# Fewer projection products kept back at the seam between the recurrence and the attention, and the first attention loads on GpSimd

## The chip, the core and the metric

The kernel runs on one core of a Trainium2 chip. Its engines are TensorE (PE in the profile, with its weight loads as PEld), VectorE (DVE), ScalarE (ACT), GpSimd (POOL) and SyncE (SP, which here only issues DMA transfers). Each engine takes its instructions in the order in which they stand in its program. The metric is the time of one execution on the device in microseconds (us). A profiled execution gives the trace that is read below; the timed runs are made without a profile.

## The reference, cut to what matters

The reference is one encoder block for 1024 tokens of width 1024, in float32. The parts around the change are the input projection, whose columns feed all branches, the first branch (a neighbourhood attention with six heads) and the second (a recurrence over time, run in both directions):

```python
h = rms_norm(x, norm_mix_g[l])
(na_q, na_k, na_v, p_r, p_k, p_v, lat_w, lat_a, lat_g, mem_q,
 gate_na, gate_rw, gate_mem) = split_columns(h @ w_in[l])
y_na = neighborhood_attention(to_heads(na_q, NA_HEADS), ...)
y_rw = rwkv7_bidirectional(p_r, p_k, p_v, lat_w, lat_a, lat_g, ...)
y_mem = memory_attention(mem_q, rms_norm(mem, norm_mem_g[l]), w_mem_kv[l])
merged = (jax.nn.sigmoid(gate_na) * (y_na @ w_branch_na[l])
          + jax.nn.sigmoid(gate_rw) * (y_rw @ w_branch_rw[l])
          + jax.nn.sigmoid(gate_mem) * (y_mem @ w_branch_mem[l]))
x = x + merged @ w_out[l]
x = x + expert_choice_ffn(rms_norm(x, norm_ffn_g[l]), ...)
```

The recurrence is a chain: every step needs the state that the step before it left.

## The kernel before, in words

The kernel works through six stages: (1) norms and the projections that the recurrence needs; (2) the recurrence, from about 350 to 826 us of the span, in which TensorE fills its waits with the other projections; (3) the attention with the group norm of the recurrence beside it, from about 853 us; (4) the merge of the branches; (5) the output projection with the router; (6) the 16 experts, whose weights are streamed.

**Products in high and low parts.** Each float32 operand is split into a high part (a copy by ScalarE, line 231) and a low part (a subtraction by VectorE, line 232), and a product is the sum of three matmuls: high by high, low by high, high by low.

**The filler.** `fill_gen` (lines 676 to 737) makes the 35 column blocks of the input projection that the recurrence does not need ("jobs"). A job has two halves of 512 tokens; each half is 24 matmuls of 128x128 by 128x512 (line 728), so that there are 1680 of these *products* in all. A step of the generator is one product. When the third product of the next half has been issued, the half before it is copied out of its PSUM bank by ScalarE (`evac`, line 716) and stored by SyncE (line 717). The two banks `acc` are used in turn, so a half cannot begin before the one two halves back has been copied out. At the seventh k step of a job's first half the weights of the next job are split (`prepw`) and those of the one after it are fetched (`load`, line 687).

**The order of the recurrence is written out by hand.** For each of its 16 units (`units`, 128 tokens of one direction) three generators are stepped round by round: `chain` of this unit (13 rounds), `t_inverse` of the next one (a triangular inverse, 31 column steps on GpSimd, then DMA transfers out to `tdr` on line 575 and back into the tile `Tbd` on line 579) and `prep` of the one after. After each round some products of the filler follow: 7 in a round until two units are left, and from there `(NFILL * 48 - RES - tail) / 28`, where `tail` is the count when that part begins (1503). With `RES` = 80 that is 3.46 a round, and 80 products are left when the last round is over; after the chain's last own matmul (line 664), 89 follow. In `chain`, line 634 is the first matmul that reads `Tbd`.

**The seam.** Lines 831 to 835 then call `na_load(0)`, the loads for the first pair of heads: its query `q` (512 KB, in two halves), the bias table of the first half of the rows (`bias_load(0)`, 960 KB) and its values `VC` (896 KB), all by SyncE, whose queue is taken in order. `na_load` goes on with the split of the query: the high parts by ScalarE (line 809), the low ones by VectorE (line 810). Only then does the loop issue the products that are left, with their copies and the split of the last job's weights. Behind them the attention begins with transposes of `VC` (line 820), scores (line 981), bias and maximum (line 987) and the exponential (line 930). `bias_load(1)` and `bias_load(2)` and the loads of the second pair of heads (`q`, `kt`, line 794) are issued by SyncE around these.

**The pool.** `ap_` holds all tiles of the attention. It takes the memory of the recurrence's pool `rp`, and a tile of it waits until the tiles that lay in its place are no longer used. Tiles are laid out in the order of their first mention.

Of the kernel before, what the change touches and what calls it, by code (L numbers as in the profile page):

```python
# [25 lines left out]
F32 = mybir.dt.float32  # L26
# [31 lines left out]
NB_ = dict(s=2, tr=2, gn=1, av=1)  # L58
PSEQ = "E A | B X | x0 | r0 | s0 o0 x1 | r1 | s1 o1 L | | T"
PRI, XTB = None, 3  # L60
NFILL, PER_ROW, TROW, PFB, RES, PRE, ROW0 = 35, 7.0, 8, 2, 80, 26, 10


def shape_constants():
# [96 lines left out]
def block_kernel(ctx: ExitStack, tc: tile.TileContext, T, out, dbg=None, upto=99):  # L161
    nc = tc.nc
    dbg = dbg or {}
    V, A, G, PE, SP = nc.vector, nc.scalar, nc.gpsimd, nc.tensor, nc.sync
# [4 lines left out]
    def scratch(name, shape):  # L169
        if name in dbg:  # L170
            return dbg[name]
        t = dram.tile(list(shape), F32, name=name)
        return t
# [24 lines left out]
    pna = scratch("pna", (6, 128, S))  # L198
    pvc = scratch("pvc", (3, 128, 16 * WSUM))
# [87 lines left out]
    with tc.tile_pool(name="wp", bufs=1, side="right", reuse_waits="tile") as wp:  # L287
# [14 lines left out]
        with (tc.tile_pool(name="qp", bufs=1, side="right", reuse_waits="tile") as qp,  # L302
# [41 lines left out]
            def mixed(d, pf, om, mu, name, bufs):  # L344
                cur, sh = (slice(1, S + 1), slice(0, S)) if d == 0 else (slice(S, 0, -1), slice(S + 1, 1, -1))
                m = qp.tile([128, S], F32, name=name, bufs=bufs)
                A.activation(m, pf[:, cur], AF.Copy, scale=om)
                V.scalar_tensor_tensor(m, pf[:, sh], mu, m, op0=OP.mult, op1=OP.add)
                return m
# [3 lines left out]
            for d in range(2):  # L353
                m = mixed(d, pf, omw[:, d:d + 1], P_("muwa", d), f"ml{d}", 1)
# [12 lines left out]
            for j in range(3):  # L367
# [3 lines left out]
                for d in range(2):  # L371
                    m = mixed(d, kf, omu[:, d * 9 + 3 + j:d * 9 + 4 + j], P_("mu", d * 9 + 3 + j), f"K{d}", 1)
# [8 lines left out]
                for d in range(2):  # L381
# [7 lines left out]
                    rb = qp.tile([128, 8, 2, 64], F32, name="rb", bufs=1)  # L389
# [19 lines left out]
                for d in range(2):  # L409
                    m = mixed(d, rf, omu[:, d * 9 + j:d * 9 + j + 1], P_("mu", d * 9 + j), "R", 1)  # L410
# [3 lines left out]
                for d in range(2):  # L414
                    m = mixed(d, vf, omu[:, d * 9 + 6 + j:d * 9 + 7 + j], P_("mu", d * 9 + 6 + j), "VV", 1)
# [353 lines left out]

    yctx = ExitStack()  # L770
    ap = yctx.enter_context(tc.tile_pool(name="ap_", bufs=1, side="right", reuse_waits="tile"))
    na, bias = {}, {}
    grid = lambda t: t.rearrange("p (r c) -> p r c", c=64)

    def bias_load(m):
        if m < 6:
            bias[m] = ap.tile([128, 2, BOFF[3]], F32, name="bias", bufs=3)
            SP.dma_start(bias[m], T["rpb"][m // 2, m % 2])

    def na_load(j):  # L780
        q = ap.tile([128, S], F32, name="q", bufs=2)
        VC = ap.tile([128, 16 * WSUM], F32, name="VC", bufs=1)
        qb = [ap.tile([128, 2, 4, 128], F32R, name=f"qb{v}", bufs=2) for v in "hl"]
        KT = kt0 if j == 0 else [(ap if j == 1 else nq).tile([128, S], F32R, name=f"KT{v}") for v in "hl"]
        na[j] = [KT, qb]
        if j == 0:
            SP.dma_start(q[:, 0:512], pna[j][:, 0:512])
            bias_load(0)
            SP.dma_start(VC, pvc[j])
            SP.dma_start(q[:, 512:], pna[j][:, 512:])  # L790
        else:
            kt = ap.tile([128, S], F32, name="kt", bufs=1)
            for t, src in ((q, pna[j]), (kt, pna[3 + j]), (VC, pvc[j])):
                SP.dma_start(t, src)
        VW = []
        for c0, ct in zip(COL0S, CTYPE):
            at, w = sum(v.shape[1] for v in VW), NCOL[ct]
            VW.append(VC[:, at:at + 16 * w])
        if j:
            yield  # L800
            yield
            for v in (slice(0, 512), slice(512, 1024)):
                A.activation(KT[0][:, v], kt[:, v], AF.Copy)
                G.tensor_tensor(KT[1][:, v], kt[:, v], KT[0][:, v].bitcast(F32), op=OP.subtract)
                yield
        for rh in range(2):
            hi, lo = (v[:, rh].rearrange("p g (r c) -> p g r c", c=16) for v in qb)
            src = q[:, 512 * rh:512 * rh + 512].rearrange("p (r g c) -> p g r c", r=8, g=4)
            A.activation(hi, src, AF.Copy)
            (G if j else V).tensor_tensor(lo, src, hi.bitcast(F32), op=OP.subtract)  # L810
            if j or rh:
                yield
        VT = ap.tile([128, 4, 4, 128], F32, name="VT", bufs=2)
        na[j].append(VT)
        for c2 in (0, 2):
            p = abank("s")
            for cg in (c2, c2 + 1):
                w = NCOL[CTYPE[cg]]
                for i in range(4):
                    PE.transpose(p[:4 * w, cg - c2, i * 128:(i + 1) * 128], VW[cg][:, 4 * i * w:4 * (i + 1) * w], ident)  # L820
            yield p, VT, c2
# [9 lines left out]
    with tc.manual_schedule():  # L831
        start = na_load(0)
        next(start)
        for _ in range(NFILL * 48 + 1 - done):
            next(fill)
    pre_ctx.close()
    pctx.close()
    aps_ctx = ExitStack()
# [311 lines left out]
    with tc.tile_pool(name="mt", bufs=1, side="right", reuse_waits="tile") as mt:  # L1150
        wq = [None, None]
        for dt_ in range(KD):
            wh, wl = wbr(dt_)
            for t0 in range(0, S, 512):
# [3 lines left out]
                m = mt.tile([128, 512], F32, name="m", bufs=1)  # L1158
                for b, (k0, n) in enumerate(((0, 3), (6, 2), (3, 3))):
# [6 lines left out]
                    else:  # L1166
                        w = mt.tile([128, 512], F32, name="u", bufs=2)
# [212 lines left out]
    with tc.tile_pool(name="eps", bufs=1, space=PSUM, reuse_waits="tile") as ps, tc.manual_schedule():  # L1380
# [93 lines left out]
        for s_ in range(steps + 1):  # L1474
# [6 lines left out]
            if s_:  # L1481
                pt = bank("tr", 2)
# [86 lines left out]
```

## Time and profile before

| what | value |
|---|---|
| median of 3 timed runs | 2369.76 us (2368.66 to 2372.98) |
| the profiled execution | 2379.35 us, its span 2377.6 us |
| busy share of the span | PE 95%, DVE 70%, ACT 55%, POOL 26% |
| mean granted clock of TensorE in that execution | 0.97 |

The span is the part of the profiled execution in which the engines work; the 1.75 us around it are the launch. "PEclk" is TensorE's granted clock as a share of 2.4 GHz: 1.00 is 2.4 GHz and 0.50 is 1.2 GHz, the two levels that appear; a value between them is a stretch with both. In rows of the timeline, the columns are the start in us, the duration in us, the engine, the line, the operation, output and input, the count, and in brackets the idle time of the engine before it with what ended that. SPq is SyncE's DMA queue; its row is the issue of a transfer, and the time that it stands there can include the wait for the transfer's conditions.

### The profile page before, as it was taken

Reading aid. Unit: us, or ns where it says so; the run is one execution under the profiler, and the core shown is the slowest. Engines: PE = TensorE matmul, PEld = TensorE weight load, DVE = VectorE, ACT = ScalarE, POOL = GpSimd, SP = SyncE. Lnnn points to the kernel's source line nnn. Section 1 sums busy time; section 2 is a strip of 40 time slices with the busy share of each in tenths; the row PEclk is TensorE's granted clock in tenths of the full one; section 3 lists DMA queues with packets and bytes.
Section 4 is the critical chain, followed back from the end, with each engine's and each line's share of the span. In section 5 each row is a group of like instructions: output and inputs, shape, how many; then the busy total and the mean of one; then the engine's idle time right before and its main releaser. Section 6 shows DMA issues by size and latency. Waiting matters only on the chain.

```text
span 2377.6 us, 33501 instructions
## 1 busy us (share of the span) xinstructions
PE 2247.3 (95%) x12494; PEld 1816.5 (76%) x12494; DVE 1665.2 (70%) x2030; ACT 1312.9 (55%) x1588; POOL 623.1 (26%) x1266
## 2 busy tenths in 40 slices
PE   7999999999999989899957999999999999999996
PEld 6677787877878756577846888888888888888885
DVE  6556556556656246564267898889888888888887
ACT  5554233333433346521235777777777777777775
POOL 1000567666666325443040000000000000000001
PEclk9999999999999998899978999999999999999998
DMA  6335444443442262075296999999999999999995
GB/s 236 151 142 208 114 115 128 127 115 105 132 123 76 80 224 98 17 233 182 93 351 243 375 379 389 385 391 383 394 381 380 380 389 386 389 387 390 379 349 195
DMA packets 196643, 594.19 MB, mean 250 GB/s; under 512 B 53376, under 2 KB 100736, under 8 KB 147328
## 3 DMA queue, kind: packets, MB, share of 16 engines
q1 hardware_dynamic: 189856, 568.62, 64.8%
q0 software_dynamic: 4752, 17.30, 2.7%
q10 hardware_dynamic: 1872, 6.13, 0.7%
q8 instruction: 98, 1.61, 0.3%
q14 instruction: 65, 0.53, 0.1%
HBM read 522.61 MB, written 69.39 MB: 249 GB/s over the span
## 4 chain that ended last, share of the span: by engine, by line
PE 51%; DVE 3%; POOL 1%; ACT 1%; issue 1%; DMA 1%; POOLq 0%; ACTq 0%; DVEq 0%
PE y L1436 14%; PE g L1424 5%; PE g L1425 5%; PE g L1427 5%; PE u L1424 5%; PE u L1425 5%; PE u L1427 5%; PE acc L235 2%; PE acc L237 1%; PE acc L236 1%; PE tr L1484 1%; POOL m L1169 1%; PE tr L1414 1%; PE pl L1256 1%; DVE ye L1342 0%
## 5 line engine op out<-in xcount | busy, mean ns | idle before, releaser
L1401 DVE TENSOR_TENSOR ewl<-raw,ewh 128x2048 fp32r<-128x2048 f32 x380 | 849.8, 2284 | 5.3 <-ACT ewh L1396 5.3
L1396 ACT ACTIVATE ewh<-raw 128x2048 fp32r<-128x2048 f32 x380 | 720.7, 1914 | 112.7 <-PE u L1425 85.2
L1443 POOL DMA_INDIRECT acc<-ye,idx x15 | 43.4, 2893 | 949.0 <-DVE ye L1442 872.1
L728 PE MATMUL acc<-hhi,wh 128*128 128x512 f32 x560 | 226.9, 405 | 3.7 <-ACT po L716 3.7
L728 PE MATMUL acc<-hhi,wl 128*128 128x512 f32 x560 | 226.9, 405 | 0.3 <-DVE wl L232 0.3
L728 PE MATMUL acc<-hlo,wh 128*128 128x512 f32 x560 | 226.5, 405 | 0.0
L568 POOL TENSOR_TENSOR tmul<-tinv,blk 96x60 f32<-96x60 f32 (+24 forms) x496 | 171.3, 345 | 147.8 <-DMA blk<-ldr 110.2
L1424 PE MATMUL g<-ewh,xh 128*128 128x512 f32 x512 | 206.0, 402 | 0.0
L1424 PE MATMUL u<-ewh,xh 128*128 128x512 f32 x512 | 202.2, 395 | 0.0
L1425 PE MATMUL g<-ewh,xl 128*128 128x512 f32 x512 | 200.2, 391 | 0.0
L1425 PE MATMUL u<-ewh,xl 128*128 128x512 f32 x512 | 199.5, 390 | 0.0
L570 POOL TENSOR_TENSOR tinv<-tinv,tmul 96x60 f32<-96x60 f32 (+24 forms) x496 | 178.5, 360 | 38.9
L1436 PE MATMUL y<-ewh,ah 128*128 128x512 f32 x512 | 137.9, 391 | 0.7 <-ACT ah L231 0.7
L1436 PE MATMUL y<-ewh,al 128*128 128x512 f32 x512 | 137.7, 391 | 0.0
L1436 PE MATMUL y<-ewl,ah 128*128 128x512 f32 x512 | 137.6, 391 | 0.0
L1427 PE MATMUL g<-ewl,xh 128*128 128x512 f32 x512 | 137.4, 390 | 0.0
L1427 PE MATMUL u<-ewl,xh 128*128 128x512 f32 x512 | 137.0, 389 | 0.0
L728 PEld LDWEIGHTS acc<-hhi,wh 128*128 128x128 f32 x560 | 107.0, 191 | 24.5 <-ACT po L716 4.1
L728 PEld LDWEIGHTS acc<-hhi,wl 128*128 128x128 f32 x560 | 106.9, 191 | 20.9 <-DVE wl L232 0.6
L728 PEld LDWEIGHTS acc<-hlo,wh 128*128 128x128 f32 x560 | 107.1, 191 | 20.6
L231 ACT ACTIVATE ah<-tr 128x512 fp32r<-128x512 f32 x64 | 38.4, 599 | 143.6 <-PE tr L1484 143.6
L232 DVE TENSOR_TENSOR wl<-wraw,wh 128x1024 fp32r<-128x1024 f32 (+1 forms) x60 | 75.5, 1263 | 54.6 <-ACT wh L231 54.5
(316 smaller groups left out, 4377.5 us busy)
## 6 DMA issues: line engine op xcount, KB each, us to landing
raw<-in_wg_dram SPq DMA_DIRECT2D x128, 1024.0 KB
raw<-in_wu_dram SPq DMA_DIRECT2D x128, 1024.0 KB
raw<-in_wd_dram SPq DMA_DIRECT2D x128, 1024.0 KB
wraw<-in_wt_dram SPq DMA_DIRECT2D x46, 512.0 KB
pt<-pz SPq DMA_DIRECT2D x16, 768.0 KB
pgt<-po SPq DMA_DIRECT2D x48, 256.0 KB
gt<-pgt SPq DMA_DIRECT2D x16, 768.0 KB
blk<-ldr SPq DMA_DIRECT2D x64, 96.0 KB
```

The source lines that it names most:

```text
L232: V.tensor_sub(lo, src, hi.bitcast(F32))
L235: PE.matmul(out_, lh, rh, start=(k_ == 0), stop=False)
L568: G.tensor_tensor(tm[:, 0:m, 0:n], tt[:, 0:m, j:j + 1].to_broadcast([4 * NB, m, n]), lt[:, j, None, j + 1:32].to_broadcast([4 * NB, m, n]) ...
L570: G.tensor_tensor(tt[:, 0:m, j + 1:32], tt[:, 0:m, j + 1:32], tm[:, 0:m, 0:n], op=OP.add)
L728: PE.matmul(p, l[:, k], r[:, k, s0:s0 + 512], start=(k == 0 and i == 0), stop=(k == KD - 1 and i == 2))
L1396: A.activation(hi, raws[seq[n]], AF.Copy)
L1401: V.tensor_sub(lo, raws.pop(seq[n]), his[seq[n]].bitcast(F32))
L1424: PE.matmul(p, xh[:, 4 * b + k], wh[:, k], start=(b == 0 and k == 0), stop=False)
L1425: PE.matmul(p, xl[:, 4 * b + k], wh[:, k], start=False, stop=False)
L1427: PE.matmul(p, xh[:, 4 * b + k], wl[:, k], start=False, stop=(b == 1 and k == 3))
L1436: PE.matmul(py[n], l[:, 2 * b + k], r[:, k, n * 512:(n + 1) * 512], start=(f == 0 and b == 0 and i == 0 and k == 0), stop=(f == 3 and b == ...
L1443: G.indirect_dma_start(out=acc[:, :], out_offset=bass.IndirectOffsetOnAxis(ap=idx[:, e:e + 1], axis=0), in_=ye, in_offset=None, compute_op ...
```

## The change

`RES` goes from 80 to 48: the last two units get 4.61 products a round in place of 3.46, and fewer are left behind the recurrence. The first three loads of the attention (`q` now in one piece, the first bias table, `VC`) are issued by GpSimd in place of SyncE. `na_load` has a `yield` behind the loads, so that the query's split is called later: after 29 of the products that are left (`n == RES // 2 + 4`). The pool mentions its tiles `sb`, `pt`, `y`, `rb` and `rq` first, so that these lie in the first places and `q`, the bias tables and `VC` elsewhere.

```diff
-NFILL, PER_ROW, TROW, PFB, RES, PRE, ROW0 = 35, 7.0, 8, 2, 80, 26, 10
+NFILL, PER_ROW, TROW, PFB, RES, PRE, ROW0 = 35, 7.0, 8, 2, 48, 26, 10
...
     ap = yctx.enter_context(tc.tile_pool(name="ap_", bufs=1, side="right", reuse_waits="tile"))
+    for nm, w, n in (("sb", 768, 4), ("pt", 768, 2), ("y", 128, 3), ("rb", 128, 2), ("rq", 128, 2)):
+        ap.tile([128, w] if w == 128 and nm != "rq" else [128, 2, w // 2], F32, name=nm, bufs=n)
...
-            SP.dma_start(bias[m], T["rpb"][m // 2, m % 2])
+            (SP if m else G).dma_start(bias[m], T["rpb"][m // 2, m % 2])
...
         if j == 0:
-            SP.dma_start(q[:, 0:512], pna[j][:, 0:512])
+            G.dma_start(q, pna[j])
             bias_load(0)
-            SP.dma_start(VC, pvc[j])
-            SP.dma_start(q[:, 512:], pna[j][:, 512:])
+            G.dma_start(VC, pvc[j])
...
+        yield
         if j:
-            yield
             yield
...
         next(start)
-        for _ in range(NFILL * 48 + 1 - done):
+        for n in range(NFILL * 48 + 1 - done):
             next(fill)
+            if n == RES // 2 + 4:
+                next(start)
```

What this moves is seen in the built programs. First TensorE in the last unit of the recurrence, from behind its first key transposes to the first matmul that reads `Tbd`. Before:

```order
L728 MATMUL acc<-hhi,wh 128x512
L728 MATMUL acc<-hhi,wl 128x512
L728 MATMUL acc<-hlo,wh 128x512
L626 MATMUL ch<-Gst,AR 64x64 x6
L728 MATMUL acc<-hhi,wh 128x512
L728 MATMUL acc<-hhi,wl 128x512
L728 MATMUL acc<-hlo,wh 128x512
L634 MATMUL ch<-u0s,Tbd_1662 128x64 x3
```

And now:

```order
L728 MATMUL acc<-hlo,wh 128x512
L728 MATMUL acc<-hhi,wh 128x512
L728 MATMUL acc<-hhi,wl 128x512
L728 MATMUL acc<-hlo,wh 128x512
L728 MATMUL acc<-hhi,wh 128x512
L626 MATMUL ch<-Gst,AR 64x64 x6
L728 MATMUL acc<-hhi,wl 128x512
L728 MATMUL acc<-hlo,wh 128x512
L728 MATMUL acc<-hhi,wh 128x512
L728 MATMUL acc<-hhi,wl 128x512
L728 MATMUL acc<-hlo,wh 128x512
L634 MATMUL ch<-u0s,Tbd_1662 128x64 x3
```

Ten products stand here where six stood. Counted over the program, the last unit but one has 14 products more (60 for 46), the last unit 12 more (46 for 34, 4 of them ahead of line 634), and 63 follow the last matmul of the chain where 89 did.

Then GpSimd, from the end of its last triangular inverse (lines 568 and 570) on. Before:

```order
L568 TENSOR_TENSOR tmul<-tinv,blk 96x8
L570 TENSOR_TENSOR tinv<-tinv,tmul 96x8
L804 TENSOR_TENSOR KTl<-kt,KTh 128x512
L873 TENSOR_TENSOR y_8836<-y_8836,y_8838 128x512
L874 TENSOR_TENSOR b_8840<-b_8840,b_8842 128x512
```

And now:

```order
L568 TENSOR_TENSOR tmul<-tinv,blk 96x8
L570 TENSOR_TENSOR tinv<-tinv,tmul 96x8
L789 DMA q<-pna 128x1024
L780 DMA bias<-in_rpb_dram 128x1920
L791 DMA VC<-pvc 128x1792
L805 TENSOR_TENSOR KTl<-kt,KTh 128x512
```

The three loads stand directly behind the inverse. By the conditions in the built program, `q` waits for nothing later than the preparation of an earlier unit, the bias table for the last unit's second key transposes (line 596), and `VC` for the matmuls behind those (line 600).

Last ScalarE, from the last copy of the recurrence (`ysb`) to the first copies of the attention. Before:

```order
L670 ACTIVATE ysb<-ch 128x3x64
L809 ACTIVATE qbh<-q 128x512 x2
L231 ACTIVATE wh<-wraw 128x1024
L716 ACTIVATE po<-acc 128x512 x4
L829 COPY VT<-s 96x512
```

And now:

```order
L670 ACTIVATE ysb<-ch 128x3x64
L716 ACTIVATE po<-acc 128x512 x2
L810 ACTIVATE qbh<-q 128x512 x2
L716 ACTIVATE po<-acc 128x512
L830 COPY VT<-s 96x512
```

The query's split has two copies of the filler ahead of it and one behind it; the split of the last job's weights (line 231) has gone up into the last unit. On SyncE, the bias tables 1 and 2 now stand behind the store of the first of these copies, and `q` and `kt` of the second pair of heads behind the store of the second.

## Rows read from the trace of the kernel before

**Rows 1.** The page: busy time of TensorE, with its share of the span and its instructions, and of the other engines.

```profile
PE 2247.3 (95%) x12494; PEld 1816.5 (76%) x12494; DVE 1665.2 (70%) x2030; ACT 1312.9 (55%) x1588; POOL 623.1 (26%) x1266
```

**Rows 2.** Stretches of 10 us around the seam: start and end, length, busy us of PE, PEld, DVE, ACT and POOL with the instructions, granted clock, busy share of the DMA engines, GB/s.

```profile
800.00:810.00 10.00, 6.87 (x45) 5.39 (x44) 0.35 (x1) 3.22 (x8) 0.00 (x0) 0.80 0.43 116
810.00:820.00 10.00, 10.00 (x86) 7.95 (x86) 2.75 (x9) 2.78 (x7) 0.00 (x0) 0.69 0.01 2
...
830.00:840.00 10.00, 6.27 (x27) 4.64 (x25) 2.43 (x3) 3.18 (x5) 0.00 (x0) 1.00 1.01 411
```

**Rows 3.** The timeline of TensorE from the end of the recurrence to the attention.

```profile
802.72 0.40 PE L728 MATMUL acc<-hlo,wh 128*128 128x512 f32 x1
...
806.25 1.51 PE L634 MATMUL ch<-u0s,Tbd 128*128 128x64 f32 x6 [3.13 <-DMA Tbd<-tdr]
...
813.88 0.91 PE L600 MATMUL tr<-cst,XV 128*64 128x64 f32 x12
...
827.68 0.39 PE L728 MATMUL acc<-hhi,wl 128*128 128x512 f32 x1
...
835.39 0.39 PE L728 MATMUL acc<-hlo,wh 128*128 128x512 f32 x1
839.46 0.49 PE L728 MATMUL acc<-hhi,wh 128*128 128x512 f32 x1 [3.69 <-ACT po L716]
840.24 0.80 PE L728 MATMUL acc<-hhi,wl 128*128 128x512 f32 x1 [0.28 <-DVE wl L232]
...
852.38 0.39 PE L728 MATMUL acc<-hlo,wh 128*128 128x512 f32 x1
853.51 1.95 PE L820 MATMUL s<-cst,VC 128*96 128x128 f32 x16 [0.74 <-ACT po L716]
```

**Rows 4.** The timeline of SyncE's DMA queue in the same stretch.

```profile
798.27 3.27 SPq L575 DMA_DIRECT2D tdr<-tinv  x4
803.05 1.78 SPq L579 DMA_DIRECT2D Tbd<-tdr  x4
...
805.36 0.48 SPq L687 DMA_DIRECT2D wraw<-in_wt_dram  x1
...
826.65 0.37 SPq L673 DMA_DIRECT2D yrw<-ysb  x1
827.12 0.43 SPq L787 DMA_DIRECT2D q<-pna  x1
...
828.57 0.42 SPq L790 DMA_DIRECT2D q<-pna  x1
...
840.80 1.21 SPq L794 DMA_DIRECT2D kt<-pna  x1
```

**Rows 5.** The timeline of ScalarE.

```profile
831.18 0.63 ACT L809 ACTIVATE qbh<-q 128x512 fp32r<-128x512 f32 x1 [4.56 <-DMA q<-pna]
837.35 0.63 ACT L809 ACTIVATE qbh<-q 128x512 fp32r<-128x512 f32 x1 [5.53 <-DMA q<-pna]
837.89 1.04 ACT L231 ACTIVATE wh<-wraw 128x1024 fp32r<-128x1024 f32 x1
838.83 1.06 ACT L716 ACTIVATE po<-acc 128x512 f32<-128x512 f32 x2
...
859.11 0.61 ACT L803 ACTIVATE KTh<-kt 128x512 fp32r<-128x512 f32 x1
...
862.34 1.06 ACT L876 ACTIVATE lg<-lg 128x1024 f32<-128x1024 f32 x1 [1.41 <-DMA lg<-plat]
```

**Rows 6.** Stretches cut at the falls of the clock (columns as in rows 2); the last is at the beginning of the attention.

```profile
806.20:816.50 10.30, 10.24 (x44) 8.54 (x44) 0.35 (x1) 2.45 (x6) 0.00 (x0) 0.51 0.28 86
...
840.20:843.70 3.50, 3.46 (x8) 2.78 (x9) 0.00 (x0) 0.00 (x0) 0.00 (x0) 0.51 1.03 311
...
864.00:871.00 7.00, 6.67 (x30) 4.22 (x30) 1.81 (x7) 4.71 (x14) 6.34 (x7) 0.51 0.80 298
```

**Rows 7.** What TensorE waited for in all of the recurrence and up to 830 us: total us, times, the longest.

```profile
PE sc L237 <- DVE rsl L232: 5.9, 16, 0.8
PE ch L634 <- DMA Tbd<-tdr: 3.1, 1, 3.1
```

**Rows 8.** The timeline of GpSimd at the end of its last triangular inverse, and its next instruction.

```profile
798.03 0.22 POOL L570 TENSOR_TENSOR tinv<-tinv,tmul 96x8 f32<-96x8 f32 x1
859.80 1.27 POOL L804 TENSOR_TENSOR KTl<-kt,KTh 128x512 fp32r<-128x512 f32 x1 [61.56 <-PE tr L995]
```

**Rows 9.** A load that GpSimd issues in this kernel, the gather of 128 rows of 4 KB for the first expert, and the matmul that waits for it.

```profile
1259.05 1.22 POOL L1406 DMA_INDIRECT xe<-h2d,idx  x1 [10.33 <-DVE tvT L1359]
...
1263.45 1.97 PE L1414 MATMUL tr<-cst,xe 128*128 128x128 f32 x8 [4.92 <-DMA xe<-h2d,idx]
```

**Rows 10.** The recurrence up to 800 us, and two stretches of 2 us: start and end, length, busy us of PE, granted clock, busy share of the DMA engines, GB/s.

```profile
350.00:800.00 450.00, 442.33 (x3504) 1.00 0.41 113
...
800.00:802.00 2.00, 2.00 (x27) 1.00 0.17 25
...
836.00:838.00 2.00, 0.00 (x0) 1.00 1.00 419
```

**Rows 11.** What TensorE waited for at the beginning of the attention, in the stretch from 820 to 900 us.

```profile
PE tr L995 <- ACT pt L999: 2.8, 3, 2.1
...
PE tr L995 <- DVE st L933: 1.3, 1, 1.3
```

## The prediction, made before the result was known

> **What bounds the kernel now.** I read the page first. TensorE is busy for 2247.3 of 2377.6 us [rows 1], so almost any time is won where it stands still or runs slowly, and the others matter where it waits for them. The stretches of 10 us come next: around the seam TensorE is busy for 6.87 us in one of them and for 6.27 in another, and the granted clock is 0.80 in the first of these and 0.69 in the full stretch behind it [rows 2], where it was 1.00 over the 450 us before [rows 10]. The timelines then say why, engine by engine, and cutting the stretches at the falls of the clock gives what these cost.
>
> There are two stalls, and each is followed by a slow stretch. In the first, TensorE ends a product at 803.12 us (802.72 and 0.40) and stands for 3.13 us until `Tbd` has landed [rows 3]. The inverse is ready at 798.25 [rows 8], SyncE writes it out from 798.27 and begins to read it back at 803.05 [rows 4]: a path of DMA alone, and too few products lie beside it. The wait is the only one of its kind in the recurrence [rows 7]. Behind it the clock is at its lower level, 1.2 GHz, for about 10 us (0.51 over 10.30 us) [rows 6]. In the second, TensorE stands for 3.69 us at 839.46 for a copy `po` of ScalarE, and 0.28 us more for the low part of the weights [rows 3]. ScalarE was not busy but held: it stood for 4.56 and 5.53 us before the two query copies, for `q`, and the copies and weight split that the filler needs stood behind these [rows 5]. `q` came late because SyncE issued it behind the store of the recurrence's last output, at 827.12 and 828.57 [rows 4]. A slow stretch follows here too, 0.51 over 3.50 us [rows 6].
>
> **The change part by part.**
>
> *Products moved ahead (RES 80 to 48).* No product is added: 1680 before and after. The pace at the full clock is 0.227 us (34 steps between 827.68 and 835.39) [rows 3]. Of the 26 moved, 14 go into the last unit but one and 4 more stand ahead of line 634, so TensorE comes to that line 18 x 0.227 = 4.1 us later, at 807.2. `Tbd` landed at 806.25 [rows 3], and its path does not hang on TensorE. The wait of 3.13 us goes, with 0.95 us to spare, and what would follow it, a slow stretch of 10.30 x (1 - 0.51) = 5.05 us [rows 6], should go with it. Up to 800 us the clock is 1.00 [rows 10] with sixteen waits of at most 0.8 us in it [rows 7], so a rest of that size would not bring the slow stretch back.
>
> *Query loaded by GpSimd.* GpSimd has nothing to do from 798.25 to 859.80 [rows 8]; its three loads stand ahead of no one else's work. `q` can be issued at 798.3. No plain load by GpSimd is in the trace. The nearest row is a gather of the same 512 KB, issued at 1259.05, whose reader begins at 1263.45 [rows 9]: 4.4 us. So `q` is there by about 803, and even three times that is 811, far ahead of its use at about 831.
>
> *Bias table and VC by GpSimd.* They wait for the last unit's second key transposes and the matmuls behind them, which began at 813.88 [rows 3]; with 18 products before them that is 818 at the latest. The two are 960 and 896 KB (128 x 1920 and 128 x 1792 floats), 1.90 MB. At the gather's 120 GB/s [rows 9] they take 15.8 us, until 834; at the 419 GB/s of a full stretch [rows 10], 4.5 us. `VC` is wanted when the products end, which the sum puts at about 838.7. No cost.
>
> *Split behind the copies.* With `q` present, and its split behind two copies, ScalarE holds nothing back. Gone are 3.69 and 0.28 us [rows 3] and the slow stretch of 3.50 x 0.49 = 1.72 us [rows 6]. The last job's weight split moves up into the last unit; its weights are issued at 805.36 [rows 4] and wanted at about 815. It costs ScalarE 1.04 us there [rows 5], beside a chain that has five products in a round to wait behind; from 0 to 1 us, taken as 0.
>
> *Second pair of heads.* This is the one thing that comes closer. `kt` was issued at 840.80 [rows 4] and first used at 859.11 [rows 5], 18 us later. Now it stands behind the store of the last half but one, some 21 products (4.8 us) before the end, so at about 835, and its first use is 6.5 us after the products' end (859.11 against 852.38 + 0.23 [rows 3, 5]), so at about 845. Ahead of it in the queues are two bias tables and a store, 2.2 MB, issued from about 828, and `q` with it; at 419 GB/s [rows 10] all of this, 3.2 MB, takes 7.7 us. It should land at about 839: nothing, with 6 us to spare.
>
> *Pool order.* It moves tiles, and adds no instruction but the place holders. The tiles put first are wanted after the recurrence is over, so it costs nothing by itself.
>
> The sum: 3.13 + 5.05 + 3.69 + 0.28 + 1.72 = 13.87 us. Against the profiled execution, 2379.35 - 13.9 = 2365.5 us. That execution is 9.6 us over the median of the timed runs. I keep the difference: 2369.76 - 13.9 = 2355.9, rounded to 2356 us. The stages behind the seam have no clock of their own: the attention and what follows begin 13.9 us earlier and run as before.
>
> *A rule that speaks against the move.* While `Tbd` is on its way the DMA engines are little used, 0.17 in 800 to 802 [rows 10]; `q` now travels just then, and at 419 GB/s its 512 KB fill them for 1.25 us. The Trainium skill (DMA: Bandwidth & Descriptors, "Issuing engines are not separate DMA queues") says that transfers of all issuing engines run on the same 16 DMA engines and interleave, so another engine's queue gives no way of its own. By that rule `Tbd` would be up to 1.25 us later, and 0.3 us of the wait would stay: 13.6 us in place of 13.9. No row has the two together.
>
> **The rivals.**
>
> *A. `Tbd` is late again.* The path of `tdr` and `Tbd` is many small transfers in turn, and `q` could cost it more than its own 1.25 us. If `Tbd` is 2 us or more late, over 1 us of waiting stays, and the slow stretch of 5.05 us with it. With all of the first stall kept, the gain is 3.69 + 0.28 + 1.72 = 5.7 us: 2364.1. For it: the margin is only 0.95 us. Against it: the first half of the way out is already issued when `q` begins to move.
>
> *B. The beginning of the attention shifts.* Before, TensorE stands there for 2.1 and 1.3 us [rows 11], ScalarE for 1.41 us for the gate's load `lg` [rows 5], and the clock is at 0.51 for 7.00 us, 3.4 us lost [rows 6]. With loads closer together, `kt` or `lg` may come some us later and add as much again, 2.1 + 3.4 = 5.5 us: 2361.4. It could as well go the other way and this stall vanish: 2350.4, which is where I end the range below.
>
> *C. Slower: `VC` comes too late by GpSimd's queue.* The bias table and `VC` stand one behind the other on one engine whose plain loads no row shows. The attention's first transposes then wait with all that follows. From 818, the gain is used up when `VC` lands at 838.7 + 13.9 = 852.6, that is at 1.90 MB in 34.6 us, 55 GB/s; under that the kernel is slower. At 40 GB/s it lands at 865.5, 12.9 us too late, and with a slow stretch of 3.4 us [rows 6] the time is 2386. Against it: 120 GB/s for the gather, whose rows lie scattered.
>
> *D. Nothing is won.* TensorE may make up for the two stalls nowhere, but something that does not hang on the seam could set the attention's end. I see no such wait: the loads of the group norm and of the merge are all issued behind work of TensorE. 2369.8.
>
> **How the numbers follow.** The forecast has a chance of 0.70, with its own range 2352 to 2360. A has 0.13, B 0.08 (later) and 0.02 (earlier), C 0.04, D 0.03. What a measurement of this kernel can tell from no change is about 0.2%, 4.7 us, so faster is under 2365.0. The forecast, B and most of A lie there: 0.70 + 0.12 + 0.07 + 0.02 = 0.91; I take 0.87, since the stalls come from one profiled execution that was 9.6 us over the timed ones. The same: 0.08; slower: 0.05. The range reaches from B's better end, 2350, to A's end with a little over it, 2365.
>
> **What would show each step.** In the profile after, line 634 has no wait in the last unit and the clock is 1.00 from 780 us to the end of the products; `qbh` waits for no DMA; no product waits for `po`; the products end at about 838.7, and the first transposes of `VC` follow within a microsecond. A wait of over 1 us at line 634 with a low clock behind it is A. A wait of `KTh` for `kt` or a longer one for `lg` is B. A wait of the first transposes for `VC` is C. The prediction is wrong if the seam is as foretold and the end is not some 14 us earlier; then the stages behind it would have taken it back.

## The result and the profile after

The changed kernel takes 2359.11 us (median of 10 runs, 2350.63 to 2365.62) where the kernel before takes 2370.78 us beside it (10 runs, 2366.49 to 2375.28). That is 11.7 us between the medians; the ratio of the two sets of runs is 0.995 with an interval of 0.9934 to 0.9967, which is 11.8 us less with 7.8 to 15.6 us as the interval. Forecast were 2356 us, 13.9 us less, which lies inside it.

The profiled execution of the changed kernel takes 2365.62 us, 13.7 us less than that of before, with a span of 2363.8 us. The page gives the busy times in the form of [rows 1]:

```profile
PE 2238.7 (95%) x12494; PEld 1810.1 (77%) x12494; DVE 1665.0 (70%) x2030; ACT 1313.0 (56%) x1588; POOL 623.9 (26%) x1269
```

The work is the same (12494 matmuls); GpSimd has the three loads more. In stretches of 10 us, with the columns of [rows 2], the holes of the seam have closed:

```profile
800.00:810.00 10.00, 9.99 (x97) 7.81 (x97) 3.54 (x9) 4.36 (x10) 0.98 (x3) 1.00 0.48 123
810.00:820.00 10.00, 10.00 (x104) 8.14 (x103) 3.38 (x10) 4.47 (x10) 1.10 (x2) 1.00 0.71 260
...
830.00:840.00 10.00, 9.88 (x44) 7.86 (x42) 1.29 (x2) 1.67 (x4) 0.00 (x0) 1.00 0.92 341
840.00:850.00 10.00, 6.38 (x49) 4.39 (x49) 6.85 (x25) 4.59 (x12) 1.27 (x1) 1.00 0.73 267
850.00:860.00 10.00, 7.71 (x44) 4.94 (x44) 1.72 (x7) 7.41 (x19) 7.11 (x8) 0.66 0.68 247
```

In the first two stretches TensorE is now busy for 9.99 and 10.00 us at a clock of 1.00, where [rows 2] had 6.87 us at 0.80 and a full stretch at 0.69; in 830 to 840 it is busy for 9.88 us and not for 6.27. The hole that is left, 840 to 860, is the beginning of the attention, which lay behind 853 before. TensorE's timeline shows the two waits of [rows 3] gone (lines of the changed kernel stand one to three numbers later from line 772 on):

```profile
808.49 0.85 PE L634 MATMUL ch<-u0s,Tbd 128*128 128x64 f32 x6
...
839.49 0.39 PE L728 MATMUL acc<-hlo,wh 128*128 128x512 f32 x1
840.61 1.95 PE L821 MATMUL s<-cst,VC 128*96 128x128 f32 x16 [0.74 <-ACT po L716]
...
848.75 0.52 PE L998 MATMUL tr<-cst,sb 128*128 128x128 f32 x3 [1.33 <-DVE st L936]
852.29 0.90 PE L998 MATMUL tr<-cst,sb 128*128 128x128 f32 x3 [3.03 <-ACT pt L1002]
```

Line 634 stands without a wait in brackets, and the products end at 839.88 (839.49 and 0.39) in place of 852.77. Of the waits at the beginning of the attention [rows 11] one has grown, from 2.1 to 3.03 us. GpSimd's timeline, which was empty here [rows 8], now has the loads:

```profile
800.09 0.21 POOL L570 TENSOR_TENSOR tinv<-tinv,tmul 96x8 f32<-96x8 f32 x1
800.63 0.76 POOL L789 DMA_DIRECT2D q<-pna  x1 [0.33 <-PE ch L654]
813.72 0.58 POOL L780 DMA_DIRECT2D bias<-in_rpb_dram  x1 [12.32 <-ACT Gst L647]
814.29 0.54 POOL L791 DMA_DIRECT2D VC<-pvc  x1
```

In the view of DMA issues, where GpSimd's loads have the time from issue to landing behind their size, two of them are

```profile
VC<-pvc POOLq DMA_DIRECT2D x1, 896.0 KB, 6.6
q<-pna POOLq DMA_DIRECT2D x1, 512.0 KB, 3.7
```

so that `q` had landed at 804.3 us and `VC` at 820.9, each long before its use. And ScalarE, which stood for 4.56 and 5.53 us before the two query copies [rows 5], makes them without a wait, but stands longer for the gate's load `lg`, 2.34 in place of 1.41 us:

```profile
835.02 1.14 ACT L810 ACTIVATE qbh<-q 128x512 fp32r<-128x512 f32 x2
...
850.30 1.06 ACT L879 ACTIVATE lg<-lg 128x1024 f32<-128x1024 f32 x1 [2.34 <-DMA lg<-plat]
```

To see where the 13.8 us of the span came from, I cut both traces at three marks: the transposes `XB` of line 596 in the last unit but one (ahead of everything that the change moves), the first transposes of `VC`, and the end of the attention's last `av`. The stretches between them, as start and end, length, busy us of TensorE, granted clock, DMA share, GB/s, are, before:

```profile
778.01:853.51 75.50, 67.66 (x495) 0.91 0.34 118
853.51:1009.90 156.39, 134.76 (x1051) 0.86 0.27 95
```

and after:

```profile
780.11:840.61 60.50, 59.76 (x494) 1.00 0.42 146
840.61:996.40 155.79, 132.66 (x1052) 0.87 0.27 96
```

The changed execution comes to the first mark 2.1 us later, before the change has touched anything. The seam is shorter by 15.0 us, the attention by 0.6, and all that follows by 0.3 (1367.7 and 1367.4 us): -2.1 + 15.0 + 0.6 + 0.3 = 13.8 us. The seam's 15.0 us are 7.10 us less standing still (75.50 - 67.66 = 7.84 before, 0.74 after) and 7.90 us less in which TensorE counts as busy.

### The profile page after: what moved, and what is told of

Same layout as the page of the kernel before. It is cut to its first block, busy times and chain, and to the rows that moved or that the text cites. A ratio compares the mean times of both kernels' runs of the same rounds, so it can differ in the third digit from the quotient of the medians.

```text
span 2363.8 us, 33505 instructions
## 1 busy us (share of the span) xinstructions
PE 2238.7 (95%) x12494; PEld 1810.1 (77%) x12494; DVE 1665.0 (70%) x2030; ACT 1313.0 (56%) x1588; POOL 623.9 (26%) x1269
## 4 chain that ended last, share of the span: by engine, by line
PE 51%; DVE 3%; DMA 1%; ACT 1%; POOL 1%; issue 1%; POOLq 0%; ACTq 0%; DVEq 0%
PE y L1439 14%; PE g L1427 5%; PE g L1428 5%; PE g L1430 5%; PE u L1427 5%; PE u L1428 5%; PE u L1430 5%; PE acc L235 2%; PE acc L237 1%; PE acc L236 1%; PE tr L1487 1%; PE tr L1417 1%; POOL m L1172 1%; PE pl L1259 1%; DVE ye L1345 0%
```

## The experiments

T1 in the expectations is the prediction's theory: the gain is the wait for `Tbd`, the wait for `po`, and the slow clock behind each. The other numbers are its rivals and the theories on single edits; what each foretells stands in the texts themselves. The table has the results of all kernels, in order of their two waits. They were timed in three groups, each with the kernel before beside it: the changed kernel first (2370.78 us for before), then e1 to e4 (2368.50), then e5, e6, e7 and a1 (2369.77); across groups the ratios can be compared and the medians can't. c1 and c2 are single executions. Waits and stretches are those of one profiled execution of each kernel. "Seam" is the first of the stretches above, "attention" the time in the second stretch in which TensorE isn't busy.

| kernel | wait for `Tbd`, us | wait for `po`, us | seam, us | attention, not busy, us | median, us | ratio to before |
|---|---|---|---|---|---|---|
| before | 3.13 | 3.69 | 75.50 | 21.6 | 2370.78 | 1 |
| before, again (c1) | 3.11 | 3.76 | 72.60 | 22.4 | 2371.15, one run | |
| before, again (c2) | 2.97 | 3.54 | 72.65 | 22.6 | 2368.91, one run | |
| e2, all but the 48 | 3.45 | none | 66.76 | 21.9 | 2366.43 | 0.9989 (0.9976 to 1.0002) |
| e1, the 48 alone | 0.25 | 1.99 | 64.64 | 22.5 | 2363.29 | 0.9971 (0.9956 to 0.9985) |
| e6, 64 kept back | 2.04 | none | 64.08 | 21.9 | 2361.26 | 0.9957 (0.9942 to 0.9973) |
| changed kernel | none | none | 60.50 | 23.1 | 2359.11 | 0.995 (0.9934 to 0.9967) |
| changed, again (a1) | none | none | 60.40 | 22.9 | 2355.22 | 0.994 (0.9922 to 0.9959) |
| e3, loads on SyncE | none | none | 60.25 | 24.8 | 2357.08 | 0.9951 (0.9936 to 0.9965) |
| e7, e3 and pool order of before | none | none | 60.33 | 24.8 | 2359.67 | 0.9956 (0.9939 to 0.9972) |
| e5, pool order of before | none | none | 60.25 | 22.4 | 2354.07 | 0.9935 (0.992 to 0.9951) |
| e4, gate's tanh later | none | none | 60.26 | 21.7 | 2357.26 | 0.9959 (0.9943 to 0.9975) |

### e1: the 48 products alone

The kernel before with one number changed:

```diff
-NFILL, PER_ROW, TROW, PFB, RES, PRE, ROW0 = 35, 7.0, 8, 2, 80, 26, 10
+NFILL, PER_ROW, TROW, PFB, RES, PRE, ROW0 = 35, 7.0, 8, 2, 48, 26, 10
```

> Only RES 80 to 48; the loads by SyncE, the split ahead of the copies and the pool order stay as before. Theory T1 (two stalls with a slow stretch each, which add up): the wait for Tbd (3.13 us) and the 5.05 us of low clock go; ScalarE is still held by q up to about 837 us, TensorE reaches the half that needs the held copy at about 834 and stands for some 3 us, with a slow stretch behind it: 8 to 9 us faster than before, about 2362. Rival T2 (the low clock is no consequence of the stall and falls somewhere else if not here): only the 3.1 us of idle time go, about 2367.5. Rival T3 (the gain comes from the loads and the pool order): no change, 2370.8.

By the ratio the time is 6.9 us less (3.6 to 10.4 us by the interval; 5.2 us between the medians). What TensorE waits for, from 780 to 841 us (total us, times, the longest):

```profile
PE acc L728 <- ACT po L716: 2.0, 1, 2.0
PE ch L634 <- DMA Tbd<-tdr: 0.2, 1, 0.2
```

The wait for `Tbd` is all but gone, and behind its 0.25 us no slow clock follows. The wait for `po` stays, though shorter than the 3.69 us of before: the second stall had lost 1.7 us by this edit alone. The seam is 8.0 us shorter than in c1 and c2 (72.6 and 64.6). Of the three theories T1 comes nearest: T3 is out, and T2's 3.1 us lie just outside the interval. But the wait for `po` was to be some 3 us and is 1.99.

### e2: everything but the 48

The changed kernel with `RES` at 80 again:

```diff
-NFILL, PER_ROW, TROW, PFB, RES, PRE, ROW0 = 35, 7.0, 8, 2, 48, 26, 10
+NFILL, PER_ROW, TROW, PFB, RES, PRE, ROW0 = 35, 7.0, 8, 2, 80, 26, 10
```

> The changed kernel with RES back at 80. T1: the wait for Tbd and its slow stretch are there again, the held copies are gone: 3.69 + 0.28 + 1.72 = 5.7 us faster than before, about 2365. T2: 4.0 us of idle time alone, about 2367. T3: nearly all of the gain, about 2359. A side question: q now moves beside Tbd, and the wait at line 634 should be between 3.1 us and, if the transfers hinder each other, 4.4 us.

The time is 2.6 us less, with an interval that reaches from 5.7 less to 0.5 more. In the trace the wait for `po` is gone and that for `Tbd` is there, with a slow stretch behind it. TensorE's timeline, and then its stretches of 2 us (start and end, length, busy us, clock, DMA share, GB/s):

```profile
804.35 0.85 PE L634 MATMUL ch<-u0s,Tbd 128*128 128x64 f32 x6 [3.45 <-DMA Tbd<-tdr]
```

```profile
804.00:806.00 2.00, 1.65 (x10) 0.91 1.08 203
806.00:808.00 2.00, 2.00 (x9) 0.50 0.70 268
808.00:810.00 2.00, 2.00 (x12) 0.74 0.00 0
810.00:812.00 2.00, 2.00 (x29) 1.00 0.20 23
```

The clock is back at 1.00 from 810 us on. Missing are 2 x (0.09 + 0.50 + 0.26) = 1.7 us, not the 5.05 us that I had put behind this wait. Its seam is 5.9 us shorter than that of c1 and c2. So the two parts by themselves bring 8.0 and 5.9 us of seam, together 13.9, and both at once 12.2 (72.6 to 60.4): the 1.7 us that e1 takes off the second stall are counted in both. The timed runs rule out T3 but don't tell T1's 5.7 us from T2's 4.0: the first lies at the edge of the interval. What speaks for T1 here is the trace, in which the slow stretch is there again. Why the runs gained less than the 5.9 us of the seam stays open.

### c1 and c2: the kernel before, profiled again

No edit. The question is whether the slow stretch of 10.30 us behind the wait for `Tbd` [rows 6] belongs to that wait.

> The kernel before, unchanged, one more profiled execution. Reading F (the 10.3 us of clock 0.51 behind the wait for Tbd belong to that wait): the same stretch again, 9.5 to 11 us at about 0.5, and the stretch from the mark of unit 14 to the first transposes of VC takes 75 to 76 us. Reading V (its length differs from execution to execution): 2 to 5 us at about 0.5, and the stretch takes 69 to 73 us.

> The kernel before, unchanged, another profiled execution. Reading F: 9.5 to 11 us at about 0.5 behind the wait for Tbd, 75 to 76 us from the mark of unit 14 to the first transposes of VC. Reading V: 2 to 5 us at about 0.5, 69 to 73 us; or a length unlike that of the execution beside it.

The first has these stretches behind its wait of 3.11 us, and this seam (columns as above):

```profile
808.00:810.00 2.00, 2.00 (x9) 0.56 0.86 260
810.00:812.00 2.00, 2.00 (x10) 0.58 0.22 84
...
778.98:851.58 72.60, 64.72 (x494) 0.95 0.36 123
```

and the second this seam:

```profile
777.39:850.04 72.65, 65.40 (x494) 0.93 0.36 121
```

Behind its wait of 3.54 us for `po`, which ended at 835.50, the second also has these stretches:

```profile
836.00:838.00 2.00, 2.00 (x5) 0.50 1.00 323
838.00:840.00 2.00, 2.00 (x6) 0.50 0.85 291
840.00:842.00 2.00, 2.00 (x9) 0.82 0.53 207
```

Reading V holds. The same wait of 3 us left a slow stretch of 10.30 us in one execution, and in c1 one that costs 2 x (0.44 + 0.42) = 1.7 us, as in e2; c2 shows the same (0.65 and 0.50 in 806 to 810, then 1.00). The slow stretch of the second stall varies too: 1.7 us were lost in the execution that I predicted from and in c1, and 2.6 us in c2 (0.5 x 0.50 = 0.25 us from 835.50 to 836, then 2 x (0.50 + 0.50 + 0.18) = 2.36 us). The seam of the execution that I predicted from was 2.9 us longer than that of the two others. Its attention was 6.1 us longer than c1's at the same work (156.39 and 150.32 us), so that seam and attention together are 9.0 us; it came to the first mark 1.0 us earlier, and was 8.2 us slower than c1 in all.

### e6: 64 products kept back

```diff
-NFILL, PER_ROW, TROW, PFB, RES, PRE, ROW0 = 35, 7.0, 8, 2, 48, 26, 10
+NFILL, PER_ROW, TROW, PFB, RES, PRE, ROW0 = 35, 7.0, 8, 2, 64, 26, 10
```

> 64 products kept back in place of 48: 9 products more than in the changed kernel stand behind line 634 and not in front of it, so TensorE comes to line 634 about 1.6 us earlier. T1 (the wait for Tbd is worth what the products in front of it leave open, and nothing else): wait at line 634 of 1.3 to 1.8 us, and 1.5 us more than the changed kernel, about 2360 us. Rival (a stretch of low clock follows any such wait, and costs as much again): 3.3 us over the changed kernel, about 2362 us, with a granted clock near 0.5 for some 3 us behind the wait. Rival (the wait is made up elsewhere): ratio as that of the changed kernel.

The waits of TensorE from 795 to 870 us, and the stretches behind the first of them:

```profile
PE ch L634 <- DMA Tbd<-tdr: 2.0, 1, 2.0
```

```profile
806.00:808.00 2.00, 2.00 (x10) 0.62 1.01 311
808.00:810.00 2.00, 2.00 (x8) 0.53 0.14 51
```

The wait is 2.04 us and the clock takes 2 x (0.38 + 0.47) = 1.7 us more, though the wait is a third shorter than in c1. Together 3.7 us, and the seam is 64.08 and not 60.40 us: 3.7 us. This is the rival of that text, the wait and about as much again; the wait itself came out longer than the 1.3 to 1.8 us that were expected. In the timed runs of the same chip it is 6.0 us over a1 by the medians, 4 us by the ratios (0.9957 and 0.994), whose intervals overlap, so that it is the trace that decides.

### e3, e5 and e7: the two other edits

e3 is the changed kernel with the three loads on SyncE:

```diff
-            (SP if m else G).dma_start(bias[m], T["rpb"][m // 2, m % 2])
+            SP.dma_start(bias[m], T["rpb"][m // 2, m % 2])
...
-            G.dma_start(q, pna[j])
+            SP.dma_start(q, pna[j])
...
-            G.dma_start(VC, pvc[j])
+            SP.dma_start(VC, pvc[j])
```

> The changed kernel with the three first loads back on SyncE; RES 48, the late split and the pool order stay. They are then issued behind the store of the recurrence's last output at about 826 us, q is there by about 830, and its split is called at about 835. T4 (the late split with fewer products is what frees ScalarE, GpSimd adds nothing): no wait for q and none for VC, same as the changed kernel within 1 us, unless the loads of the second pair of heads come late: they now stand behind the last store of the filler, 5 us later than in the changed kernel, so kt may be 1 to 4 us late for KTh, which with a slow stretch costs up to 5 us: 2359 to 2364. T5 (GpSimd is needed): q or VC is waited for again by ScalarE or TensorE for 3 us or more, 2364 or over.

e5 is the changed kernel without the place holders of the pool:

```diff
-    for nm, w, n in (("sb", 768, 4), ("pt", 768, 2), ("y", 128, 3), ("rb", 128, 2), ("rq", 128, 2)):
-        ap.tile([128, w] if w == 128 and nm != "rq" else [128, 2, w // 2], F32, name=nm, bufs=n)
```

> The changed kernel without the place holders that reserve sb, pt, y, rb and rq first, so q, bias and VC lie again where they lay before. Each of the three tiles then shares memory with tiles of the last unit: q waits for line 640 of that unit's second half, bias behind it on GpSimd, VC for the end of the chain. T4 (order not needed): the loads are issued at about 821 to 826 us in place of 801 and 814, still land by about 833, in front of the first copies of q at 835, and the seam is as in the changed kernel; ratio to the kernel before 0.994 to 0.996, 2357 to 2359 us. T6 (the order is what makes room): q or VC lands behind 835 us, TensorE waits 2 us or more at the first transposes of VC or the first scores, 2362 us or over.

e7 takes both back, so that 48 products and the later split are left.

> The kernel before with two of the four edits: 48 products kept back, and the split of q behind the first group's copies (with the start stepped at product 28 of the last call). The loads stay on SyncE (q whole) and the pool order is that of before. T4 (the two edits are the whole gain): no wait at line 634, none for po, ratio 0.994 to 0.996, about 2357 to 2359 us. T6 (each of the other two covers for the other): q, or VC, or the gather on SyncE's queue comes late, a wait of 2 us or more at the first transposes of VC or the first scores, 2362 us or over.

All three have the seam of the changed kernel, 60.25 to 60.33 us, and neither of the two waits. In e5 GpSimd issues its loads as late as foretold:

```profile
817.44 0.76 POOL L787 DMA_DIRECT2D q<-pna  x1 [21.47 <-ACT u0s L642]
818.19 0.58 POOL L778 DMA_DIRECT2D bias<-in_rpb_dram  x1
822.53 0.54 POOL L789 DMA_DIRECT2D VC<-pvc  x1 [3.76 <-DVE Gst L657]
```

and it is as fast as the changed kernel beside it (2354.07 and 2355.22 us, ratios 0.9935 and 0.994 with intervals that overlap). Behind the seam the loads on SyncE do leave a trace. ScalarE in e7:

```profile
844.75 0.63 ACT L802 ACTIVATE KTh<-kt 128x512 fp32r<-128x512 f32 x1 [2.03 <-DMA kt<-pna]
...
848.77 1.06 ACT L877 ACTIVATE lg<-lg 128x1024 f32<-128x1024 f32 x1 [2.20 <-DMA lg<-plat]
```

and what TensorE waits for there, from 820 to 900 us (line 996 of e7 is line 998 of the changed kernel):

```profile
PE tr L996 <- ACT pt L1000: 5.6, 2, 3.8
...
PE tr L996 <- ACT sb L931: 2.1, 1, 2.1
```

`kt` is 2.03 us late, where the changed kernel has no such wait, and the two long waits at the beginning of the attention are 3.8 and 2.1 us in place of 3.03 and 1.33. In e3 it is 0.81 us for `kt` and 2.92 us for `lg`. TensorE stands for 24.8 us in the attention of both, and for 22.4 to 23.1 us in e5, a1 and the changed kernel. So T4 holds for the seam: the number of products and the place of the split are the gain, and neither GpSimd nor the pool order is needed for it. One part was not taken back alone: all these kernels load `q` in one piece ahead of `VC`, where the kernel before loads its second half behind `VC`. That an early `q` with the split in its old place would have done as well is not ruled out either. That GpSimd's queue saves some 2 us further on is what the traces say, one of each kernel; the timed runs are compatible with that (0.9951 and 0.9956 against 0.9935 to 0.995) but don't show it, since all their intervals overlap.

### e4: the gate's tanh moved

In the changed kernel ScalarE stands for `lg` ahead of work that TensorE wants. Here the pair of instructions on `lg` is moved behind the group norm's first steps:

```diff
-            if n == 0:
-                A.activation(lg, lg, AF.Tanh, scale=0.5)
-                G.tensor_scalar(lg, lg, 0.5, 0.5, op0=OP.mult, op1=OP.add)
...
+            if n == 0:
+                A.activation(lg, lg, AF.Tanh, scale=0.5)
+                G.tensor_scalar(lg, lg, 0.5, 0.5, op0=OP.mult, op1=OP.add)
```

> The changed kernel with one thing more: ScalarE's tanh of the gate latents lg (and GpSimd's scaling behind it) is called some seven steps later, ahead of its only reader, so that ScalarE does not stand for lg at the beginning of the attention. Rival B of the prediction says that this stall (2.34 us on ScalarE, 3.03 us on TensorE, then a clock of 0.66 over 10 us) is worth about 5 us: 2354, with TensorE's longest wait there under 1.5 us and no fall of the clock behind it. If the low clock there has another cause: 2357. If the stall moves to the next load (y of the group norm, KTh): 2359, no gain.

The wait for `lg` goes, and with it the 3.03 us; in their place TensorE's waits from 820 to 900 us have the group norm, which waits for its own load:

```profile
PE gn L881 <- POOL y L876: 2.1, 1, 2.1
...
PE tr L998 <- ACT pt L1002: 1.0, 2, 0.7
```

The attention has 21.7 us of standing, 1.1 to 1.4 us less than a1 and the changed kernel, and the time (0.9959, 0.9943 to 0.9975) is no better. That is the third case of the text, the stall that moves to the next load, though the new wait is the shorter one. Nothing that was tried beats the changed kernel by more than the measurement tells.

### a1: the changed kernel again

> The changed kernel once more, timed on the same chip as the three beside it. All theories: ratio 0.993 to 0.997. What it tells: whether the clock behind the last product (0.66 to 1.00 in the ten microseconds behind 850 us) and the entry into the stretch (780 us) repeat, or differ from execution to execution by 2 to 4 us.

The seam and the attention, as above:

```profile
777.22:837.62 60.40, 59.66 (x495) 1.00 0.42 147
837.62:987.90 150.28, 127.43 (x1052) 0.92 0.29 99
```

The seam repeats to 0.1 us. The attention does not: 150.28 us against 155.79 in the first execution, with the same standing (22.9 and 23.1 us) but a clock of 0.92 and not 0.87. Before, it is the same: 156.39 us at 0.86, and 150.32 at 0.91 in c1. So one pair of profiles can be 6 us apart in the attention by its clock alone, and the entry into the seam lay between 775.8 and 780.1 us over all kernels of the table.

## Why the prediction was right, and where a size was off

**The two stalls.** They were the gain, as forecast. The sum had 3.13 + 3.69 + 0.28 = 7.10 us of standing; in the profile TensorE stands for 7.84 us in the seam before and 0.74 after, which is 7.10. e1 and e2 each remove one of them and keep the other, e1 not cleanly. In the six profiles that have neither wait (the changed kernel, a1, e3, e4, e5, e7) the clock is 1.00 all through the seam; each of the six that has one shows a slow stretch behind it.

**The slow clock behind the first stall: mis-sized.** The step that was off is "10.30 x (1 - 0.51) = 5.05 us". It is right for the one execution that I read, and c1, c2, e2 and e6 show 1.7 us behind the same wait. That it "should go with it" holds: after, the clock is 1.00 all through the seam. Measured from the 72.6 us of c1 and c2, and not from 75.5, the seam gains 12.2 us; the attention stands about 0.5 us longer (22.9 and 23.1 us in a1 and the changed kernel, 22.4 and 22.6 in c1 and c2). The timed runs say 11.8, with 7.8 to 15.6 as the interval, so they can't tell the forecast's 13.9 from that, and by its clock the attention differs by more than these 2 us from one profile to the next. The forecast noted that its execution lay 9.6 us over the median, and carried the whole 13.9 us over to the median nevertheless.

**What the sum did not have.** Eighteen products ahead of line 634 were to bring TensorE there 4.1 us later, "with 0.95 us to spare". Counted from the first mark it comes there 3.3 us later (28.4 against 25.1 us). Counted in the two traces, the products do take 4.1 us more, but the chain's small matmuls between them take 0.8 us less. The twelve of line 626 in the last unit, before and after:

```profile
801.38 0.84 PE L626 MATMUL ch<-Gst,AR 128*64 128x64 f32 x12
```

```profile
806.54 0.57 PE L626 MATMUL ch<-Gst,AR 128*64 128x64 f32 x12
```

With three products ahead of them they take 0.84 us, with five 0.57, and neither row has a wait in brackets. So part of the products went into time that the profile counted as busy; what the small matmuls stood for in it the rows don't say. Over the whole seam, from the start of each small matmul to the start of the next instruction, without the waits and with half of the time at the lower clock taken off, I count in the traces 18.6, 18.8 and 18.8 us for the kernel before, c1 and c2, and 17.6 us for the changed kernel and a1. These 1.0 to 1.2 us are a gain that no row of waits shows, and with them the seam adds up: against a1, c1 has 7.1 us of standing, 3.4 us of slow clock and 1.2 us of this, 11.7 of 12.2 us; c2 has 6.5, 4.3 and 1.1, 11.9 of 12.25 us. The forecast came near because one term was too large and another was missing, and that part of its closeness is luck.

**No spare.** For the same reason the 0.95 us did not exist. From the issue of `tdr` to the start of line 634 it takes 8.16 us in the changed kernel without a wait, and 7.96 to 8.32 us in the kernels that do wait there; e7 comes there after 7.95 us and does not wait. SyncE's rows of the changed kernel, to be laid beside [rows 4]:

```profile
800.33 3.27 SPq L575 DMA_DIRECT2D tdr<-tinv  x4
805.10 1.78 SPq L579 DMA_DIRECT2D Tbd<-tdr  x4
...
836.05 0.40 SPq L795 DMA_DIRECT2D kt<-pna  x1
...
843.44 0.42 SPq L857 DMA_DIRECT2D lg<-plat  x1
```

The number 48 just reaches, with next to nothing to spare; e1 has it too and waits for 0.25 us, and e6, nine products fewer, pays 3.7 us. The forecast was right here by luck: had the wait been 1 us and not 0, rival A might have come in part.

**The rule on queues.** `q`, 512 KB, travels beside `tdr` alone: in the changed kernel it landed at 804.3 us, and `Tbd` was issued from 805.10 on; in the others that load it there it also landed ahead of `Tbd`. From the first issue of `tdr` to the first of `Tbd` it takes 4.77 to 4.78 us in the seven kernels without `q` there (before, c1, c2, e1, e3, e5, e7), and 4.77 to 5.00 us in the five with it (the changed kernel, a1, e2, e4, e6), 0.08 us more on the mean. The Trainium skill (DMA: Bandwidth & Descriptors, "Issuing engines are not separate DMA queues") says that such transfers share the 16 engines and interleave. These runs don't contradict it, but the up to 1.25 us that I had worked out from it, a transfer that goes ahead as a whole, is far above the measured cost.

**Query, bias table and `VC`.** No wait for any of them after, as forecast. The reason given was too broad: e3 and e7 have none either, with the loads in SyncE's queue. What the kernels without a wait have in common is that the split no longer stands ahead of ScalarE's copies (and that `q` comes in one piece); who issues the loads doesn't matter there. The bounds for GpSimd's loads were wide: `q` landed 3.7 us after its issue (the gather had given 4.4), and `VC` at 820.9 us, where the slower estimate had 834.

**The beginning of the attention.** Rival B, if it came in at all, came in small. `kt` was forecast at about 835 and is issued at 836.05, and its copy does not wait. But `lg` is late by 2.34 us and not 1.41, and TensorE's long wait grew from 2.1 to 3.03 us. SyncE issues `lg` at 843.44, 3.56 us behind the end of the products (before: 856.38, 3.61 us behind it), and ScalarE can begin 6.86 us after that (850.30), where it was 5.96 us before (862.34). So the load itself takes longer, 0.9 us in this pair. That this comes of the change is not shown: ScalarE waits for `lg` for 1.73 us in c1 and in a1, and TensorE's long wait is 2.4 us in both. Nor are the loads that came closer, as B had it, seen to be the cause: between 842 and 844 us, when `lg` was issued, the DMA engines moved only 54 GB/s. e4 shows that this price cannot be had back by moving the tanh alone, since TensorE then waits for the group norm, whose load comes late as well.

**Rivals A, C and D.** A's wait is not there. C needed `VC` to land after the products' end, by 13.9 us to use up the gain; it landed 19 us ahead of that end, and TensorE's row at 840.61 waits for `po`. D fell with the end of the attention, which came 13.5 us earlier; behind it before and after differ by 0.3 us.

## What to carry to other kernels

A stall of the engine that bounds the kernel is best taken from the profile in two parts, the wait itself, which repeats to a few tenths, and the slow clock behind it, which was three times as long here in one execution as in the next. The second needs more than one profiled execution before it goes into a sum. When work is moved in front of a wait, ask whether part of it falls into time that already counts as busy: it then costs less, but also delays the waiting engine less, and a margin worked out from it is too large. And an edit of several parts is worth taking apart: here one number and the place of one call (with `q` loaded in one piece) were the whole gain that could be measured.

## What the runs showed of the hardware that was not expected

The length of the slow stretch does not follow the length of the wait. At line 634 waits of 2.04, 2.97, 3.11 and 3.45 us each cost 1.7 us of clock behind them, one of 3.13 us cost 5.05 us, and one of 0.25 us (e1) nothing. Of the waits for `po`, 3.69 and 3.76 us cost 1.7 us, 3.54 us (c2) cost 2.6 us. A wait of 1.99 us (e1, for `po`) is among those that cost 1.7 us too: the clock is 0.58 in the 4 us behind it.

```profile
836.00:840.00 4.00, 4.00 (x11) 0.58 0.92 277
```

And two executions of the same instructions with the same standing time can differ by 5.5 us in 155 (a1 and the changed kernel's first profile) because the clock is granted differently over the attention.
